# LayerNorms 2 and 3 with statistics from transposed token blocks, and two sets of first weights split at an earlier place in the program

## The chip, the cores and the metric

The kernel runs on one core of a Trainium2 chip. The metric is the time of one execution on the device in microseconds (us). Before the change the median of three runs is 2775.86 us (2774.26 to 2776.49).

## The reference, cut to what matters

One encoder layer is applied to two groups of 512 tokens (prompt and sample) with shared weights, model width 1024, all in fp32:

```
x = LN1(alpha*x + 0.5*SwiGLU_1(x))
h = x @ W_in                                  # columns for MLA, RWKV-7 and gates
A = MLA(h) @ P_mla ;  B = RWKV7_bidir(h) @ P_rwkv
x = LN2(alpha*x + (sig(g_A)*A + sig(g_B)*B) @ W_o)
x = LN3(alpha*x + CrossAttn(x, LN(mem)))
x = LN4(alpha*x + 0.5*SwiGLU_2(x))

def _layernorm(x, g, b):
    mu = mean(x, -1); var = mean((x - mu)**2, -1)
    return (x - mu) * rsqrt(var + 1e-5) * g + b
```

A LayerNorm needs the mean and variance of each token over its 1024 features.

## The kernel before, in words

**Layout.** Activations lie transposed: features on the 128 partitions, 512 tokens along a row. A group's activation is eight rows (`KT` = 8) of 128 x 512. Each fp32 operand of a product is split into a high part, rounded to fp32r by ScalarE (a CAST, line 246), and a low part, the difference, made by VectorE or GpSimd (line 247, which the profile shows as L180 where VectorE is called through the wrapper `Held`). A product is three matmuls of 128x128 by 128x512 (`Bank.prod`, matmuls at L216): high x high, high x low, low x high. Results collect in eight PSUM banks, four with tag `a`, two with `b`, two with `c`. Tile names in the profile: `xh`, `xl` are the parts of normalized rows, `wraw` a raw weight slot, `whl` its two parts, `wt` a sum of weight blocks, `ps` a bank, `cc` the constants with the identity.

**Weights.** The projections and everything up to the cross-attention output read their weights from a `Stream`. `Stream.fetch` takes a raw buffer (pool `w`: 2 buffers) and a split buffer (`whl`, pool `w`: 3 buffers, one more in another pool), issues a load of 512 KB on SP's queue (L142) and the two split instructions. `next_slot` calls `fetch` when a slot is asked for and none is ready. The feed-forward's weights come from `FfnWeights`, a generator with the same buffers; `next()` keeps up to `AHEAD` = 3 tiles of lead, and `ahead(n)` runs the generator n steps before they are asked for (loads at L459). The first feed-forward uses it while the input is loaded.

**Order.** The program is written as one list of instructions. A planner lays down each engine's order before the run: it keeps a model of time, and of the instructions whose inputs and buffers the model has ready it takes the one that stands first in the program. So a later line can run ahead of an earlier one, and each engine then works through its own list in that order. `order(...)` adds an edge by hand; `k.after`, set by `BlockNorm.stats(..., True)`, puts all later VectorE instructions behind the end of that statistic.

**The stages around the change, in order of time.**

1. *First feed-forward* (`ffn`). Its last loop, `down_step` over `DOWN`, makes seven block products a step by Strassen's scheme. The last step (`final`) takes its products in the order 1 2 6 5 3 7 4; `ahead(i)` is called before the i-th.
2. *LayerNorm 1* is a `BlockNorm`. `add(half)` handles four rows: for each of four token blocks, four transposes of 128 x 128 on TensorE into one bank (L221), then one `bn_stats` on VectorE over the bank. `stats` joins the halves (`bn_aggr`), makes the reciprocal root by three Newton steps of small VectorE instructions (`rstd_of`), and `spread` brings scale and shift back to the transposed layout by eight transposes. `applying` then does, for each row: multiply and add on VectorE, gain and bias on ScalarE (L359), high part on ScalarE, low part on GpSimd.
3. *Projections.* `compressed(2, ..., decay)` takes three weight slots and runs them abreast: for each row of a group the nine matmuls of the three slots, first group 0, then group 1. At its end ScalarE copies the banks (L1002).
4. Recurrence, attention and their outputs.
5. *LayerNorm 2* over `mix_row`, and *LayerNorm 3* over `out_rows`. Both are `RowNorm`: after each row ScalarE squares it (L375), VectorE adds the square to one sum (`ln_s`), and GpSimd (group 0, L378) or VectorE (group 1) adds the row to another. `stats` reduces the two sums over the partitions by eight fp32 matmuls with a column of 1/1024 (`k.mean`; the profile has sixteen records a group).
6. Cross attention: `both(attend(1), out_rows(0))` interleaves group 1's attention with group 0's output rows; `out_rows(1)` follows, then the rows of LayerNorm 3.
7. *Second feed-forward*: the same `ffn` with `last=True`. It asks for its first four weight slots by `fw.next()`, and runs them abreast over group 0's rows of LayerNorm 3, then over group 1's.

Of the kernel before, what the change touches and what calls it, by code (L numbers as in the profile page):

```python
# [11 lines left out]
F32 = mybir.dt.float32  # L12
F32R = mybir.dt.float32r
I32 = mybir.dt.int32
AF = mybir.ActivationFunctionType
ALU = mybir.AluOpType
# [4 lines left out]
P = 128  # L21
# [342 lines left out]
            yield  # L364


class RowNorm(Norm):


    def add(self, n):  # L370
        nc, y = self.k.nc, self.y(n)
        if n == 0:
            self.s1, self.s2 = self.tile("ln_s1", 2), self.tile("ln_s2", 2)
        sq = self.tile("sq", 4) if n else self.s2
        nc.scalar.activation(out=sq, in_=y, func=AF.Square)  # L375
        if n:
            eng = nc.gpsimd if self.tags[0] == "c" else nc.vector
            eng.tensor_tensor(out=self.s1, in0=self.s1 if n > 1 else self.y(0), in1=y, op=ALU.add)  # L378
            nc.vector.tensor_tensor(out=self.s2, in0=self.s2, in1=sq, op=ALU.add)

    def stats(self):
        k, nc, sb = self.k, self.k.nc, self.sb
        st = Bank(k, self.tags[0])
        for o, t in enumerate((self.s1, self.s2)):
            for b in range(4):
                st.mm(st.t[:, 4 * o + b : 4 * o + b + 1], t[:, b * P : b * P + P], k.mean)
        m = sb.tile([P, 3, 4], F32, name="ln_m", tag="ln_m", bufs=2)
        mean, var, sq = m[:, 0], m[:, 1], m[:, 2]
        nc.vector.tensor_copy(m[:, 0:2], st.t[:, 0:8].rearrange("p (a b) -> p a b", b=4))
        nc.vector.scalar_tensor_tensor(out=sq, in0=mean, scalar=-1.0, in1=mean, op0=ALU.mult, op1=ALU.mult)  # L390
        nc.vector.scalar_tensor_tensor(out=var, in0=sq, scalar=LN_EPS / ALPHA**2, in1=var, op0=ALU.add, op1=ALU.add)
        Norm.spread([self], mean, var)


class BlockNorm(Norm):


# [129 lines left out]
            ra, rb = nxt  # L527


def ffn(k, fw, x32, std, rows_of, op_tile, posts, sums, d_h, d_s, norm_of, applied, last=False):  # L530

# [50 lines left out]
    def down_step(n, u2, u4):  # L584
        m, p0, p1_ = DOWN[n]

        def ahead(i):

            if i == 2 and m == 3:
                while due:  # L590
                    due.pop(0)()
            if i == 2:
                for p in range(p1_, max([p1_, *(b for _, _, b in DOWN[n + 1 : n + 2])])):
                    fetch(p)

        ps, done = {}, set()
        y = {(r, c): x32[:, rows_of[r], 2 * m + c] for r in range(2) for c in range(2)}

        def add(out, name, u):
            nc.vector.scalar_tensor_tensor(out=out, in0=ps[name].t, scalar=SC, in1=u, op0=ALU.mult, op1=ALU.add)  # L600

        final = n == len(DOWN) - 1

        def more(r, c, u):

            eng = nc.vector if final else nc.gpsimd
            eng.tensor_tensor(out=y[r, c], in0=y[r, c], in1=u, op=ALU.add)  # L607

        def to_y(r, c, name, u):
            add(y[r, c], name, y[r, c])  # L610
            if not final:
                more(r, c, u)

        def summed(i, x):

            x.add(m // 2)
            if m == 3 and not last:
                if i == 1:  # L620
                    going.append(applied(rows_of[0], norms[0]))
                    for _ in range(3):
                        next(going[0])
                BlockNorm.stats([x], True)
            elif m == 3 and i == 1:
                BlockNorm.stats(norms, True)

        todo = [
            ("p1", "1", lambda: nc.scalar.activation(out=u2, in_=ps["1"].t, func=AF.Identity, scale=SC)),
            ("c11", ("2", "p1"), lambda: to_y(0, 0, "2", u2)),  # L630
            ("u2", ("6", "c11"), lambda: add(u2, "6", u2)),
            ("u4", ("5", "u2"), lambda: add(u4, "5", u2)),
            ("u3", ("7", "u4"), lambda: add(u2, "7", u2)),
            ("c22", ("7", "u4"), lambda: to_y(1, 1, "7", u4)),
            ("c12", ("3", "u4"), lambda: to_y(0, 1, "3", u4)),
            ("c21", ("4", "u3"), lambda: to_y(1, 0, "4", u2)),
        ]
        if final:
            for name, (r, c, of, u) in {"d11": (0, 0, "p1", u2), "d12": (0, 1, "u4", u4), "d22": (1, 1, "u4", u4),
                                        "d21": (1, 0, "u3", u2)}.items():  # L640
                todo.insert(0, (name, (of,), lambda r=r, c=c, u=u: more(r, c, u)))
            todo = [(a, (*b, "d" + a[1:]) if a[0] == "c" else b, f) for a, b, f in todo]
        if p1_ == NP and m == 3:
            for r, x in enumerate(norms):
                todo.append((f"n{r}", (f"c{r + 1}1", f"c{r + 1}2"), lambda r=r, x=x: summed(r, x)))
        elif p1_ == NP and m == 1:
            due.extend(lambda r=r, x=x: summed(r, x) for r, x in enumerate(norms))
        strassen(k, fw, turn_of(n), ps, done, todo, p1_ - p0,
                 lambda o, i: tuple(slot(OPS.index(o), (p0 + i) % 4)[:, j] for j in range(2)), ahead)


    with posts() as sb:
# [13 lines left out]
        for g in range(G):  # L666
            xp = [std[g].pair(i) for i in range(KT)]
            banks = [Bank(k, "a") for _ in range(4)]
            ws = [[(o[0][:, i * P : i * P + P], o[1][:, i * P : i * P + P]) for i in range(KT)] for o in w]
            if last:  # L670
                abreast(banks, ws, xp)
            for j in range(2):
                pg, pu = banks[2 * j : 2 * j + 2]
                if not last:
                    for b, o in zip((pg, pu), ws[2 * j : 2 * j + 2]):
                        b.prod(b.t, list(zip(o, xp)))
                s = sb.tile([P, 2, T], F32, name="s", tag="s", bufs=2)[:, 0]
                nc.scalar.activation(out=s, in_=pg.t, func=AF.Silu)
                nc.vector.tensor_tensor(out=s, in0=s, in1=pu.t, op=ALU.mult)
                to_h(s, d_s[j][g], sb)  # L680
# [122 lines left out]
def kernel(  # L803
# [55 lines left out]
    nc.vector.memset(k.ones, 1.0)  # L859
    k.half = cp.tile([P, 1], F32, name="half")  # L860
    nc.vector.memset(k.half, 0.5)
    k.mean = cp.tile([P, 1], F32, name="mean")
    nc.vector.memset(k.mean, 1.0 / D)
    vc = cp.tile([P, NVEC], F32, name="vc")
    nc.sync.dma_start(out=vc, in_=vec)

# [31 lines left out]
    with ExitStack() as f1:  # L898
# [35 lines left out]

        places = {n: (xpools[0], "x", 4) for n in ("A11", "A12")}
        places.update({n: (xpools[1], "x", 4) for n in ("A22", "S4")}, **{n: (xo, "xo", 6) for n in ("S1", "S2", "S3")})
        ffn(k, fw, x32, xs, (0, 1), op_tiles(places), lambda: pool("post1"), sums1, d_h, d_s, norm1, applied1)

    def gate_out(n, g, h, t):
        nc.scalar.activation(out=t, in_=h, func=AF.Tanh, scale=0.5, bias=hbg[:, n : n + 1])  # L940
# [364 lines left out]
    y32 = keep.tile([P, G, KT, T], F32, name="x32")  # L1305
    x32 = [y32[:, g] for g in range(G)]

    def norms_of(i):
        return [RowNorm(k, sb, lambda n, g=g: x32[g][:, n], f"ln{i}_g", f"ln{i}_b", "cb"[g] * 2) for g in range(G)]

    for q in range(4):
        for g in range(G):
            nc.sync.dma_start(out=x32[g][:, 2 * q : 2 * q + 2], in_=d_x1[g][:, 2 * q : 2 * q + 2])
    wb_pool = cross.enter_context(pool("wb", "right"))
    st.use((wp, 3, 2), (wb_pool, 2, 0), (wp, 3, 2), (wb_pool, 2, 0), (wp, 3, 2))

    def sum_row(norm, g, n, b, f):
        y = x32[g][:, n]
        nc.vector.scalar_tensor_tensor(out=y, in0=b.t, scalar=f, in1=y, op0=ALU.mult, op1=ALU.add)
        norm.add(n)  # L1320

    norms = norms_of(2)
    w = []

    def mix_row(g, n):
# [4 lines left out]
    for n0 in (0, 4):  # L1330
        w += [st.blocks(KT) for _ in range(4)]
        for g in range(G):
            for n in range(n0, n0 + 4):
                mix_row(g, n)
            if (n0, g) == (4, 0):
                norms[0].stats()
    x2 = [None, None]
    for g in range(G):
        if g:
            norms[g].stats()  # L1340
        x2[g] = (acts if g else others)(KT, "x")
        norms[g].apply(x2[g])

# [79 lines left out]
    kvs[1] = memory_of(1)  # L1423
    xo[1] = acts(4, "co")
    w = [st.blocks(4) for _ in range(KT)]
    norms = norms_of(3)
    both(attend(1), out_rows(0))
    norms[0].stats()
    for _ in out_rows(1):
        pass  # L1430
    x3 = [None, None]
    for g in range(G):
        if g:
            norms[g].stats()
        x3[g] = acts(KT, "x")
        norms[g].apply(x3[g])


    cross.close()
    ow, of = ctx.enter_context(pool("ow", "right")), ctx.enter_context(pool("of"))  # L1440
    fw = FfnWeights(k, wf2, [(wp, 3)] * 3 + [(ow, 1)], [(wp, 2)] * 2 + [(ow, 1)], ow)
    ln = []

    def sums2():
# [8 lines left out]

    places = {n: (mixed, "xs", 8) for n in ("A11", "A12", "A22", "S4")}
    places.update({n: (keep, "xs", 4) for n in ("S1", "S2")}, S3=(of, "xo", 2))
    ffn(k, fw, y32, x3, (1, 0), op_tiles(places), lambda: pool("post2"), sums2, d_h, d_s, norm4, applied4, True)


def softmax(k, sb, s, scale):
# [544 lines left out]
```

## Time and profile before

| what | value |
|---|---|
| median of three runs | 2775.86 us |
| the profiled execution, its time | 2775.84 us |
| its span, first to last instruction | 2774.1 us |
| mean granted TensorE clock | 0.963 |
| TensorE busy | 2605.6 us, 94% |
| VectorE busy | 2123.8 us, 77% |
| ScalarE busy | 1095.9 us, 40% |
| GpSimd busy | 699.1 us, 25% |

The profiled execution agrees with the median to 0.02 us, and its span is 1.7 us shorter than its time. In the rows below, a timeline row gives the start in us from the span's start, the duration, the engine (PE = TensorE, DVE = VectorE, ACT = ScalarE, POOL = GpSimd, SPq = SP's queue), the line, the operation, output and inputs, shapes, and the count of merged instructions; brackets give how long the engine stood before it and what ended that. A group row gives busy us and the mean ns of one, then idle time before it. A matmul's duration includes its way through the array: in a dense stream the next one starts before it ends, so costs on TensorE are read from starts.

### The profile page before, as it was taken

Reading aid. Unit: us, or ns where it says so; the run is one execution under the profiler, and the core shown is the slowest. Engines: PE = TensorE matmul, PEld = TensorE weight load, DVE = VectorE, ACT = ScalarE, POOL = GpSimd, SP = SyncE. Lnnn points to the kernel's source line nnn. Section 1 sums busy time; section 2 is a strip of 40 time slices with the busy share of each in tenths; the row PEclk is TensorE's granted clock in tenths of the full one; section 3 lists DMA queues with packets and bytes.
Section 4 is the critical chain, followed back from the end, with each engine's and each line's share of the span. In section 5 each row is a group of like instructions: output and inputs, shape, how many; then the busy total and the mean of one; then the engine's idle time right before and its main releaser. Section 6 shows DMA issues by size and latency. Waiting matters only on the chain.

```text
span 2774.1 us, 41500 instructions
## 1 busy us (share of the span) xinstructions
PE 2605.6 (94%) x15600; PEld 2079.9 (75%) x15600; DVE 2123.8 (77%) x3749; ACT 1095.9 (40%) x2008; POOL 699.1 (25%) x479
## 2 busy tenths in 40 slices
PE   8999999997899999997989888899999999999996
PEld 7888887785767777776777676677777888887784
DVE  7888887999366777758475768656798888887987
ACT  5334342223353555444443432224554343342222
POOL 0323332443100001133133321103032332332443
PEclk9999999999989999998899898999999999999998
DMA  4344437661244333343434354441101433447751
GB/s 171 130 150 160 152 145 296 235 235 57 95 165 150 112 106 111 111 143 129 131 109 131 119 178 126 161 174 42 54 31 67 161 144 138 152 162 267 273 202 68
DMA packets 164776, 398.18 MB, mean 144 GB/s; under 512 B 41120, under 2 KB 47520, under 8 KB 164576
## 3 DMA queue, kind: packets, MB, share of 16 engines
q1 hardware_dynamic: 164576, 395.53, 40.8%
q8 instruction: 124, 2.03, 0.3%
q14 instruction: 76, 0.62, 0.1%
HBM read 261.50 MB, written 133.96 MB: 143 GB/s over the span
## 4 chain that ended last, share of the span: by engine, by line
PE 76%; DVE 15%; ACT 3%; issue 2%; DMA 2%; POOL 1%; SPq 0%; POOLq 0%; ACTq 0%; DVEq 0%
PE ps L216 73%; PE ps L221 3%; DVE whl L180 2%; DVE dw L180 2%; DVE z L180 1%; DVE x L180 1%; DVE tm L180 1%; DVE rs L180 1%; DVE wt L180 1%; DVE s L180 1%; DVE ln_s L180 1%; DVE phi L180 1%; ACT whl L246 0%; DMA ld<-d_rw 0%; DVE up L180 0%
## 5 line engine op out<-in xcount | busy, mean ns | idle before, releaser
L216 PE MATMUL ps<-xh,whl 128*128 128x512 f32 x2688 | 890.2, 402 | 26.7 <-DVE whl L180 16.8
L216 PE MATMUL ps<-xo,whl 128*128 128x512 f32 x3792 | 899.7, 396 | 14.2 <-DVE z L180 8.5
L216 PEld LDWEIGHTS ps<-xo,whl 128*128 128x128 f32 x3792 | 713.0, 189 | 185.6 <-DVE z L180 6.7
L216 PEld LDWEIGHTS ps<-xh,whl 128*128 128x128 f32 x2688 | 507.8, 190 | 144.2 <-DVE whl L180 20.4
L216 PE MATMUL ps<-xl,whl 128*128 128x512 f32 x1344 | 535.1, 399 | 1.5 <-POOL xl L247 1.5
L180 DVE TENSOR_TENSOR whl<-wraw,whl 128x512 fp32r<-128x512 f32 (+4 forms) x273 | 282.5, 1045 | 63.6 <-ACT whl L246 62.9
L246 ACT CAST whl<-wraw 128x512 fp32r<-128x512 f32 (+4 forms) x318 | 223.9, 715 | 250.1 <-PE ps L216 210.8
L216 PEld LDWEIGHTS ps<-xl,whl 128*128 128x128 f32 x1344 | 255.8, 190 | 55.8 <-POOL xl L247 2.3
L709 POOL TENSOR_TENSOR s<-s,up 128x512 f32<-128x512 f32 x80 | 115.9, 1449 | 626.6 <-DVE up L180 391.1
L246 ACT CAST whl<-wt 128x512 fp32r<-128x512 f32 (+3 forms) x280 | 148.5, 555 | 276.0 <-PE ps L216 164.1
L180 DVE TENSOR_TENSOR whl<-wt,whl 128x512 fp32r<-128x512 f32 (+3 forms) x280 | 216.7, 795 | 10.8 <-ACT whl L246 10.3
L247 POOL TENSOR_TENSOR whl<-wraw,whl 128x1024 fp32r<-128x1024 f32 x45 | 109.1, 2426 | 385.5 <-ACT whl L246 355.4
L246 ACT CAST hop<-s 128x512 fp32r<-128x512 f32 x128 | 79.5, 621 | 238.2 <-POOL s L709 178.0
L180 DVE TENSOR_TENSOR hop<-s,hop 128x512 fp32r<-128x512 f32 x128 | 121.4, 949 | 55.4 <-ACT hop L246 48.0
L180 DVE SCALAR_TENSOR_TENSOR x<-ps,x 128x512 f32<-128x512 f32 x184 | 124.5, 683 | 50.6 <-PE ps L216 50.2
L180 DVE TENSOR_TENSOR wt<-wraw 128x512 f32<-128x512 f32 (+3 forms) x140 | 110.6, 791 | 1.0
L180 DVE TENSOR_TENSOR wt<-wraw,wt 128x512 f32<-128x512 f32 (+3 forms) x140 | 103.1, 737 | 4.2 <-DMA wraw<-in_wf_dram 2.1
L607 POOL TENSOR_TENSOR x<-x,s 128x512 f32<-128x512 f32 x48 | 70.7, 1478 | 129.4 <-DVE x L180 129.4
L247 POOL TENSOR_TENSOR xl<-x,xh 128x512 fp32r<-128x512 f32 x48 | 68.6, 1453 | 91.8 <-ACT xh L246 91.5
L180 DVE TENSOR_TENSOR p<-ps,p 128x512 f32<-128x512 f32 x120 | 82.2, 685 | 7.8 <-PE ps L216 4.8
L607 POOL TENSOR_TENSOR x<-x,z 128x512 f32<-128x512 f32 x48 | 71.3, 1486 | 52.8 <-DVE x L180 49.2
L216 PE MATMUL ps<-mh,whl 128*128 128x512 f32 x256 | 82.2, 401 | 0.0
(328 smaller groups left out, 3728.2 us busy)
## 6 DMA issues: line engine op xcount, KB each, us to landing
d_h<-hop SPq DMA_DIRECT2D x140, 512.0 KB, 2.6
xo<-d_h SPq DMA_DIRECT2D x140, 512.0 KB, 7.2
wraw<-in_wf_dram SPq DMA_DIRECT2D x95, 512.0 KB, 3.4
wraw<-in_wa_dram SPq DMA_DIRECT2D x57, 512.0 KB, 3.5
wraw<-in_wb_dram SPq DMA_DIRECT2D x36, 512.0 KB, 3.4
wraw<-in_wf_dram SPq DMA_DIRECT2D x36, 384.0 KB, 3.9
ld<-d_rw SPq DMA_DIRECT2D x24, 512.0 KB, 4.7
d_gate<-t SPq DMA_DIRECT2D x32, 256.0 KB, 2.4
```

Source lines behind the costliest of these rows:

```text
L180: inst = f(*args, **kw)
L216: self.last = order(k.tc, k.nc.tensor.matmul(out, a, b, start=start, stop=stop), self.last)
L221: self.last = order(self.k.tc, self.k.nc.tensor.transpose(out, a, ident), self.last)
L246: nc.scalar.copy(hi, src)
L247: (low or nc.vector).tensor_tensor(out=lo, in0=src, in1=hi.bitcast(F32), op=ALU.subtract)
L607: eng.tensor_tensor(out=y[r, c], in0=y[r, c], in1=u, op=ALU.add)
L709: nc.gpsimd.tensor_tensor(out=s[:, i], in0=s[:, i], in1=up[:, i], op=ALU.mult)
```

## The change

`RowNorm` is removed, and `norms_of` makes `BlockNorm`s with bank tags for transposes and spreading. The rows call `add` once for each four rows. In the first feed-forward's last step, before its fifth product, `early` fetches the first three slots of the projections' stream. The second feed-forward's `FfnWeights` and the pool `ow` are made before `out_rows(1)`, and three of its four first slots are generated after the fourth, sixth and eighth row of group 1. `ffn`'s flag `last` becomes `early`, with the opposite sense.

```diff
-class RowNorm(Norm):
-    def add(self, n):
...
-    def stats(self):
...
-def ffn(k, fw, x32, std, rows_of, op_tile, posts, sums, d_h, d_s, norm_of, applied, last=False):
+def ffn(k, fw, x32, std, rows_of, op_tile, posts, sums, d_h, d_s, norm_of, applied, early=None):
...
+        final = n == len(DOWN) - 1
+
         def ahead(i):
 
             if i == 2 and m == 3:
                 while due:
                     due.pop(0)()
+            if i == 4 and final and early:
+                early()
...
-            if m == 3 and not last:
+            if m == 3 and early:
...
-            if last:
+            if not early:
                 abreast(banks, ws, xp)
...
-    k.mean = cp.tile([P, 1], F32, name="mean")
-    nc.vector.memset(k.mean, 1.0 / D)
...
-        ffn(k, fw, x32, xs, (0, 1), op_tiles(places), lambda: pool("post1"), sums1, d_h, d_s, norm1, applied1)
+        ffn(k, fw, x32, xs, (0, 1), op_tiles(places), lambda: pool("post1"), sums1, d_h, d_s, norm1, applied1,
+            lambda: [st.fetch() for _ in range(3)])
...
-    def norms_of(i):
-        return [RowNorm(k, sb, lambda n, g=g: x32[g][:, n], f"ln{i}_g", f"ln{i}_b", "cb"[g] * 2) for g in range(G)]
+    def norms_of(i, *tags):
+        return [BlockNorm(k, sb, lambda n, g=g: x32[g][:, n], f"ln{i}_g", f"ln{i}_b", tags[g]) for g in range(G)]
...
+    ow = ctx.enter_context(pool("ow", "right"))
...
-        norm.add(n)
-
-    norms = norms_of(2)
+        if n % 4 == 3:
+            norm.add(n // 4)
+
+    norms = norms_of(2, ("c", "b"), ("c", "c"))
...
-                norms[0].stats()
+                BlockNorm.stats(norms[:1], False)
...
-            norms[g].stats()
+            BlockNorm.stats(norms[1:], False)
...
-    norms = norms_of(3)
+    norms = norms_of(3, ("a", "b"), ("c", "c"))
     both(attend(1), out_rows(0))
-    norms[0].stats()
-    for _ in out_rows(1):
-        pass
+    BlockNorm.stats(norms[:1], False)
+    fw = FfnWeights(k, wf2, [(wp, 3)] * 3 + [(ow, 1)], [(wp, 2)] * 2 + [(ow, 1)], ow)
+    for i, _ in enumerate(out_rows(1)):
+        if i % 4 == 3 and i > 4:
+            fw.ahead(1)
...
     cross.close()
-    ow, of = ctx.enter_context(pool("ow", "right")), ctx.enter_context(pool("of"))
-    fw = FfnWeights(k, wf2, [(wp, 3)] * 3 + [(ow, 1)], [(wp, 2)] * 2 + [(ow, 1)], ow)
+    of = ctx.enter_context(pool("of"))
```

More of the change, by code (lines that the diff above doesn't have):

```diff
@@ L364, in applying @@
             yield
-class RowNorm(Norm):
-    def add(self, n):
[L371 to L379, printed above, removed]
-    def stats(self):
[L382 to L392, printed above, removed]
 class BlockNorm(Norm):
@@ L600, in add @@
             nc.vector.scalar_tensor_tensor(out=out, in0=ps[name].t, scalar=SC, in1=u, op0=ALU.mult, op1=ALU.add)
-        final = n == len(DOWN) - 1
         def more(r, c, u):
@@ L673, in ffn @@
                 pg, pu = banks[2 * j : 2 * j + 2]
-                if not last:
+                if early:
                     for b, o in zip((pg, pu), ws[2 * j : 2 * j + 2]):
@@ L1433 @@
         if g:
-            norms[g].stats()
+            BlockNorm.stats(norms[1:], False)
         x3[g] = acts(KT, "x")
@@ L1455 @@
     places.update({n: (keep, "xs", 4) for n in ("S1", "S2")}, S3=(of, "xo", 2))
-    ffn(k, fw, y32, x3, (1, 0), op_tiles(places), lambda: pool("post2"), sums2, d_h, d_s, norm4, applied4, True)
+    ffn(k, fw, y32, x3, (1, 0), op_tiles(places), lambda: pool("post2"), sums2, d_h, d_s, norm4, applied4)
 def softmax(k, sb, s, scale):
```

## The prediction

> **What bounds the kernel now.** I read the page first (busy times, chain), then the waits of TensorE, then the timelines of each engine at the four places that the diff touches, then windows for the granted clock.
>
> ```profile
> span 2774.1 us, 41500 instructions
> PE 2605.6 (94%) x15600; PEld 2079.9 (75%) x15600; DVE 2123.8 (77%) x3749; ACT 1095.9 (40%) x2008; POOL 699.1 (25%) x479
> ...
> PE 76%; DVE 15%; ACT 3%; issue 2%; DMA 2%; POOL 1%; SPq 0%; POOLq 0%; ACTq 0%; DVEq 0%
> ...
> PE ps L216 <- DVE whl L180: 18.9, 5, 14.3
> ```
>
> TensorE is busy 94% of the span and makes 76% of the chain that ended last. So time is won only where TensorE stands, and each instruction put on TensorE in a dense stretch costs its full spacing. The last row is of the waits: five waits of matmuls for a weight split on VectorE are 18.9 us, and one of them is 14.3 us. It lies at the start of the projections:
>
> ```profile
> 678.35 0.40 PE L216 MATMUL ps<-xl,whl 128*128 128x512 f32 x1
> 684.45 1.09 PE L221 MATMUL ps<-cc,ln_v 128*128 128x128 f32 x4 [5.70 <-DVE ln_v L180]
> ...
> 700.71 1.22 PE L216 MATMUL ps<-xh,whl 128*128 128x512 f32 x2 [14.32 <-DVE whl L180]
> ...
> 638.07 14.53 SPq L142 DMA_DIRECT2D wraw<-in_wa_dram  x2
> 700.68 0.33 SPq L142 DMA_DIRECT2D wraw<-in_wa_dram  x1
> ...
> 661.82 1.05 ACT L246 CAST whl<-wraw 128x1024 fp32r<-128x1024 f32 x1 [7.96 <-PE ps L216]
> ...
> 699.37 1.29 DVE L180 TENSOR_TENSOR whl<-wraw,whl 128x1024 fp32r<-128x1024 f32 x1
> ...
> 701.18 1.70 DVE L180 TENSOR_TENSOR whl<-wraw,whl 128x1024 fp32r<-128x1024 f32 x1
> ...
> 688.43 18.08 POOL L247 TENSOR_TENSOR xl<-x,xh 128x512 fp32r<-128x512 f32 x13 [5.72 <-ACT xh L246]
> ...
> 734.52 0.59 ACT L1002 COPY c<-ps 128x512 f32<-128x512 f32 x1 [10.59 <-PE ps L216]
> ```
>
> Two of the first three weight slots were loaded from 638, and the second was cast by 662.9. Yet their low halves are made on VectorE only at 699.37 and 701.18, among the last rows of LayerNorm 1, and the third slot is loaded only then, since it reuses the raw buffer of the first. The normalized rows are there much earlier: GpSimd makes the low halves of the last thirteen rows from 688.43 on, 1.39 us each (18.08/13). Row 3 of the first token group is complete at 689.8, and the last row of the second at 706.5. The copy at 734.52 tells when the first three projections (3 slots x 16 rows x 3 = 144 matmuls) ended, at 734.4.
>
> ```profile
> 640.00:678.00 38.00, 31.22 (x167) 24.61 (x166) 35.38 (x65) 6.93 (x10) 9.76 (x6) 1.00 0.07 24
> 680.43:704.33 23.90, 5.41 (x15) 3.90 (x16) 22.07 (x40) 17.16 (x28) 18.10 (x14) 0.50 0.47 184
> 707.00:740.00 33.00, 32.52 (x142) 26.49 (x142) 8.76 (x12) 10.53 (x17) 0.21 (x2) 1.00 0.20 65
> 1895.58:1898.99 3.41, 3.41 (x10) 2.63 (x9) 2.11 (x13) 0.00 (x0) 0.00 (x0) 0.50 0.00 0
> 2062.83:2076.49 13.66, 10.99 (x34) 8.10 (x34) 13.23 (x27) 4.05 (x7) 5.66 (x3) 0.50 0.43 136
> ```
>
> In these windows the columns are TensorE, weight loads, VectorE, ScalarE, GpSimd, then granted clock. Where TensorE stood, the clock fell to 0.50 and stayed there for some us after work came back. In the dense window 142 matmuls take 33 us, 0.233 us each.
>
> The second place is the start of the second feed-forward:
>
> ```profile
> 2059.15 0.39 PE L216 MATMUL ps<-xh,whl 128*128 128x512 f32 x1
> ...
> 2062.12 2.96 PE L216 MATMUL ps<-mean,ln_s 128*128 128x1 f32 x16 [0.35 <-DVE ln_s L180]
> 2066.47 2.00 PE L216 MATMUL ps<-xh,whl 128*128 128x512 f32 x3 [1.39 <-DVE whl L180]
> ...
> 2096.20 0.50 PE L216 MATMUL ps<-xh,whl 128*128 128x512 f32 x1 [0.28 <-DVE s L180]
> ...
> 2048.10 1.05 ACT L246 CAST whl<-wraw 128x1024 fp32r<-128x1024 f32 x1 [0.92 <-PE ps L216]
> ...
> 2064.39 0.68 DVE L180 TENSOR_TENSOR s<-s,ps 128x512 f32<-128x512 f32 x1
> ...
> 2065.20 1.22 DVE L180 TENSOR_TENSOR whl<-wraw,whl 128x1024 fp32r<-128x1024 f32 x1
> ...
> 2073.16 1.23 DVE L180 TENSOR_TENSOR whl<-wraw,whl 128x1024 fp32r<-128x1024 f32 x1
> ...
> 2116.23 0.69 DVE L180 TENSOR_TENSOR s<-s,ps 128x512 f32<-128x512 f32 x1 [9.83 <-PE ps L216]
> ```
>
> The same picture, smaller. The first group's 4 x 24 = 96 matmuls need 22.4 us, but run from 2059.15 to 2096.20, 37 us. The second slot's cast was done at 2049.2; the four low halves came on VectorE from 2065.20 to 2074.4, behind the rows of group 0 (until 2065.1) and between the links of group 1's statistics.
>
> **The change, part by part.**
>
> *Transposed blocks (LayerNorms 2 and 3).* The trace has their price at LayerNorm 1, which does just this:
>
> ```profile
> L221 PE MATMUL ps<-cc,x 128*128 128x128 f32 x64 | 9.7, 277 | 2.8 <-DVE ln_b L180 2.1 <-DVE x L180 0.7
> L180 DVE BATCH_NORM_STATS2 ln_b<-ps 128x6 f32<-128x512 f32 x16 | 10.6, 689 | 0.7 <-PE ps L221 0.6
> ...
> 657.14 0.60 PE L221 MATMUL ps<-cc,x 128*128 128x128 f32 x4
> 657.50 0.95 PE L216 MATMUL ps<-xo,whl 128*128 128x512 f32 x3
> 658.29 0.38 PE L221 MATMUL ps<-cc,x 128*128 128x128 f32 x2
> ...
> 1892.48 1.05 PE L216 MATMUL ps<-mean,ln_s 128*128 128x1 f32 x8 [0.57 <-POOL ln_s L378]
> 1893.39 0.47 PE L216 MATMUL ps<-ml,whl 128*128 128x512 f32 x1
> ...
> 1894.17 0.95 PE L216 MATMUL ps<-mean,ln_s 128*128 128x1 f32 x8
> 1894.98 0.47 PE L216 MATMUL ps<-ml,whl 128*128 128x512 f32 x1
> ...
> L180 DVE TENSOR_TENSOR ln_s<-ln_s,sq 128x512 f32<-128x512 f32 x28 | 28.0, 1001 | 5.8 <-ACT sq L375 5.5
> ```
>
> Four transposes of one bank hold TensorE from 657.14 to 657.50, 0.36 us; the three matmuls behind them take 0.79 instead of 0.70. So a bank costs 0.45 us. A LayerNorm of two groups fills 16 banks: 7.2 us, or 14.4 for both. What goes is the sums by matmul: 0.91 + 0.81 us of stream, two restarts of 0.09 and the wait of 0.57, so 2.5 us for this group. I take the same for group 1: 4.9 for LayerNorm 2. Its net is +2.3. In LayerNorm 3, group 0 pays 3.6 and saves 1.9, group 1's first half pays 1.8, and the second half lies in the stall counted below. Together +5.8, say **+6**, on the dense path. Bounds: +1 (the 1.7 us of the half-clock window that follows those sums at 1895.58 goes too, and waits with them) to +11 (also the idle 2.8/16 us a bank, and no saving in LayerNorm 3).
>
> VectorE loses 28 additions of 1.0 us and the twelve of group 1's first sum, and gets 32 statistics of 0.69 us (22 us) and 16 small ones. ScalarE loses 32 squares, GpSimd its sums. None of these bounds the dense stretch, so nothing there, covered by TensorE. The memset of `k.mean` at the start goes: nothing, beside the first loads.
>
> The trace calls a transpose 277 ns long, three times its spacing. The Trainium skill, page "TensorE: Matmul & The Clock Gate", section "Part 4: PE-mode transpose", gives about 275 ns in a kernel's context, which agrees as a duration. Were it occupancy, 128 of them would cost 35 us instead of 14.4 and the whole sum would be +3 us, 2778; the starts at 657.14 and 657.50 decide against it.
>
> *Projections' weights.* `early` issues three loads and six split halves at the fifth of the last step's seven products, so ahead of LayerNorm 1 in program order. Nothing is added; each is moved past the last sums, both statistics, sixteen rows and, on SP, the eight stores of d_x1. VectorE is busy 35.38 of 38 us in 640:678, so the low halves cost there: two of 1.2 us fit partly in its 2.6 idle us; the third needs a buffer that the last products hold, comes near 674 and delays the rows by 1.2. I take 1.7 us of delay for the rows (bounds 0 and 3.7, three whole splits). The three casts find ScalarE busy 6.93 of those 38 us. On SP the loads pass stores that are read back only in the recurrence's filling work: nothing, even if the third load's wait for a raw buffer holds them. The VectorE time freed at 699.37 to 702.9 goes to the last rows.
>
> What is late next: the rows. The three slots run abreast, nine matmuls a row, 2.1 us, slower than rows arrive (1.39). The 27 matmuls of rows 0 to 2 run before 689; the other 117 start when row 3 is there, 689.8 + 1.7 = 691.5, and need 27.3 us, 718.8. One clock window at half (1.7) and one bank turnover (0.6) make 721. Against 734.4 that is **-13**. Bounds: -16 (no delay, full clock) and -7 (3.7 us delay and two more half-clock windows).
>
> *Second feed-forward's weights.* Three of the four slots are split in program order within group 1's output rows. The first two follow their casts, the third still waits for the last row's matmul to free its buffer. VectorE between 2041 and 2060 drops fourteen additions of 0.6 us spacing, gains four statistics and two splits of 1.2: about 4 us less, so group 0's rows end near 2061 instead of 2065.1. Then TensorE has 48 matmuls (11 us) for two slots at 2059.15 and the rest as they come: 2059.15 + 22.4 + 1.8 (four banks) + 0.8 (eight spreads) = 2084.2; with 1 us of waits 2085.2 against 2096.2, **-11**. Bounds: -12 and -5 (VectorE stays behind, clock stays at half). Is it given back by the operand sums on VectorE? It idles 9.83 us before 2116.23, so 11 us less on TensorE and about 5 us less on its own side still fit. The `ow` pool opened earlier is space, no time.
>
> *Sum.* +6 - 13 - 11 = -18 us. The profiled execution took 2775.84, as the median 2775.86: **2757.8**. 0.2%, 5.6 us, is about what a measurement of this kernel tells from no change.
>
> **Rivals.**
> 1. *Only one of the two starts is won.* For: each engine's order is laid down before the run, and splits already sit far behind their casts (661.82 to 701.18). Against: both now stand ahead of the norms in the program. -13 + 6 gives 2769, -11 + 6 gives 2771.
> 2. *Slower: the banks stall TensorE.* Most norms rotate two banks, each freed by a 0.69 us statistic. If TensorE stood 0.9 us for each of the 28 banks in dense stretches: +25, 2783. It decides from (18 + 5.6)/28 = 0.84 us a bank; against it, 2.8 us of idle stood before 16 banks in LayerNorm 1, 0.18 each.
> 3. *Clock.* A burst of small instructions drops the clock: the half-speed window at 1895.58 comes right after sixteen of them. One window costs 1.7 us; seven dense half-norms, 12 us: 2770. Against: 64 transposes in 640:678 at clock 1.00. The same section of that page says that transposes do not count as busy for the clock; the 640:678 window does not bear it out.
> 4. *The splits stay where they were* (the change does not do what it says): +6, 2782.
> 5. *More*: both starts and the norms at their good bounds, -16 - 12 + 1 = -27, 2749; half of it 2752.
>
> **How the numbers follow.** Forecast 0.62 (own range 2753 to 2766), rival 1 0.14, rival 2 0.05, rival 3 0.05, rival 4 0.04, rival 5 0.10. Faster by over 0.2% (below 2770.3): the forecast, rival 5, half of rivals 1 and 3, 0.81. Slower (above 2781.4): rivals 2 and 4, less 0.01, 0.08. Same 0.11. The range 2750 to 2771 leaves out rivals 2 and 4, parts of 1 and 3 and the end of 5.
>
> **What would show it.** Right: no wait near 14 us before the first projections, their 144 matmuls ending 13 us sooner after the last product; low halves on VectorE before LayerNorm 1's rows; group 0 of the second feed-forward in about 26 us instead of 37, at clock 1.0; 128 more transposes, dense stretches of LayerNorms 2 and 3 about 6 us longer. Wrong: splits still among the rows; gaps of 0.8 us before transposes; half-clock windows inside LayerNorm 2; a new wait for operand sums after the feed-forward's first blocks.

## The result, and the profile after

| | median, us | runs, us | ratio to the kernel before |
|---|---|---|---|
| before | 2776.18 | 2774.26 to 2776.51 | |
| after | 2747.59 | 2745.05 to 2753.66 | 0.9902 [0.9884, 0.9919] |

The change wins 28.6 us where 18 were forecast; the median lies 2.4 us below the range. The profiled execution is the slowest of its four, 2753.66 us (22.2 us won), so stages are compared below over several kernels' traces, too.

The page of the changed kernel, its span, busy times and the shares of the chain that ended last:

```profile
span 2751.4 us, 41550 instructions
...
PE 2601.3 (95%) x15664; PEld 2085.6 (76%) x15664; DVE 2113.7 (77%) x3746; ACT 1075.5 (39%) x1976; POOL 677.1 (25%) x465
...
PE 54%; DVE 11%; issue 3%; ACT 3%; DMA 2%; POOL 1%; SPq 1%; POOLq 0%; ACTq 0%; DVEq 0%
```

TensorE is busy for about as many us as before. The start of the projections, in the timeline, its waits and a window (columns as in the prediction):

```profile
661.75 1.21 DVE L180 TENSOR_TENSOR whl<-wraw,whl 128x1024 fp32r<-128x1024 f32 x1
666.04 1.23 DVE L180 TENSOR_TENSOR whl<-wraw,whl 128x1024 fp32r<-128x1024 f32 x1
676.47 1.21 DVE L180 TENSOR_TENSOR whl<-wraw,whl 128x1024 fp32r<-128x1024 f32 x1
...
690.08 0.62 PE L221 MATMUL ps<-cc,ln_v 128*128 128x128 f32 x4 [0.92 <-DVE ln_v L180]
694.03 0.97 PE L216 MATMUL ps<-xh,whl 128*128 128x512 f32 x3 [1.04 <-ACT xh L246]
712.48 0.98 PE L216 MATMUL ps<-xh,whl 128*128 128x512 f32 x2 [2.48 <-ACT xh L246]
...
724.84 0.59 ACT L977 COPY c<-ps 128x512 f32<-128x512 f32 x1 [4.53 <-PE ps L216]
...
PE ps L216 <- DVE whl L180: 3.3, 2, 2.8
...
690.00:718.00 28.00, 24.01 (x98) 18.68 (x99) 22.31 (x31) 18.96 (x31) 17.05 (x15) 0.94 0.44 162
```

The low halves stand ahead of LayerNorm 1's rows, the wait of 14.3 us is gone, and the copy that stood at 734.52 stands at 724.84. (The 2.8 us left in that list of waits lie elsewhere.) The start of the second feed-forward:

```profile
2030.66 1.23 DVE L180 TENSOR_TENSOR whl<-wraw,whl 128x1024 fp32r<-128x1024 f32 x1
2037.60 1.21 DVE L180 TENSOR_TENSOR whl<-wraw,whl 128x1024 fp32r<-128x1024 f32 x1
2047.34 2.27 DVE L180 TENSOR_TENSOR whl<-wraw,whl 128x1024 fp32r<-128x1024 f32 x1
2050.13 1.95 DVE L180 TENSOR_TENSOR whl<-wraw,whl 128x1024 fp32r<-128x1024 f32 x1
...
2048.44 0.48 PE L216 MATMUL ps<-xh,whl 128*128 128x512 f32 x1
2052.13 0.97 PE L216 MATMUL ps<-xh,whl 128*128 128x512 f32 x3 [0.50 <-DVE whl L180]
2074.90 0.50 PE L216 MATMUL ps<-xh,whl 128*128 128x512 f32 x1 [0.71 <-ACT s L654]
2077.36 0.50 PE L216 MATMUL ps<-xh,whl 128*128 128x512 f32 x1 [0.80 <-DVE s L180]
...
2048.00:2075.00 27.00, 25.61 (x122) 20.15 (x120) 26.13 (x51) 14.70 (x22) 11.36 (x9) 1.00 0.12 39
```

The row that stood at 2096.20 before (a wait for `s`) is the one at 2077.36. From the first product it comes 28.9 us later (2077.36 - 2048.44) instead of 37.1 (2096.20 - 2059.15), and the clock stays at 1.00. In both traces 102 products lie in that stretch, group 0's 96 and six of group 1. The 96 alone took 35.2 us before (the 97th starts at 2094.35) and 25.6 now (they end at 2074.0; the 97th is the one at 2074.90).

The next table shows how far each trace is ahead of the kernel before, in us. It compares the starts of the same instructions of VectorE, ScalarE, GpSimd and of the DMA issues, before minus now, as the median over those that started in the 20 us from the time named (in the time of the kernel before). In column 2020, where ScalarE's rows changed their order, the value is VectorE's. The runs e0 to e14 are described below.

| from | 640 (last step of FFN 1) | 740 (projections) | 1440 | 1820 (recurrence over) | 1920 (LN 2 over) | 2020 (attention over) | 2100 (FFN 2 under way) | 2760 (end) |
|---|---|---|---|---|---|---|---|---|
| after | -2.2 | 9.7 | 13.4 | 9.9 | 10.3 | 12.5 | 18.6 | 22.6 |
| e0, the same kernel | -1.1 | 13.4 | 15.4 | 11.5 | 12.6 | 14.9 | 21.0 | 24.9 |
| e5, without the splits ahead | -1.0 | 15.5 | 19.3 | 18.5 | 19.9 | 22.2 | 28.1 | 30.7 |
| e6, after with the old places | -0.5 | 16.1 | 16.0 | 18.9 | 18.7 | 20.6 | 26.5 | 26.3 |
| e10, norms alone, old places | -2.7 | -2.7 | -1.7 | -6.4 | -6.3 | -4.3 | 1.2 | 0.8 |
| e2, early projections alone | -0.7 | 15.4 | 16.9 | 10.7 | 11.1 | 12.7 | 11.3 | 11.1 |

Read across, the same steps recur: 12 to 17 us at the projections' start where `early` is in; 5.5 to 6.1 us between 2020 and 2100 wherever the norms are in; about 2 us in the attention, but 1.6 in e2 as well, which has the old norms; and 2.6 to 4 us within the second feed-forward in after, e0 and e5, but not in e6 and e10. Between 1440 and 1820 the traces move by -6.2 to +2.9 in no order that follows the change: the same program moved by -3.5 (after) and -3.9 (e0). The cause of that scatter stays open.

### The profile page after: what moved, and what is told of

Read it like the earlier page. It is cut to its first block, busy times and chain, and to the rows that moved or that the text cites. A ratio compares the mean times of both kernels' runs of the same rounds, so it can differ in the third digit from the quotient of the medians.

```text
span 2751.4 us, 41550 instructions
## 1 busy us (share of the span) xinstructions
PE 2601.3 (95%) x15664; PEld 2085.6 (76%) x15664; DVE 2113.7 (77%) x3746; ACT 1075.5 (39%) x1976; POOL 677.1 (25%) x465
## 4 chain that ended last, share of the span: by engine, by line
PE 54%; DVE 11%; issue 3%; ACT 3%; DMA 2%; POOL 1%; SPq 1%; POOLq 0%; ACTq 0%; DVEq 0%
PE ps L216 51%; PE ps L221 3%; DVE whl L180 1%; DVE z L180 1%; DVE dw L180 1%; DVE x L180 1%; DVE tm L180 1%; DMA ld<-d_rw 1%; DVE rs L180 1%; DVE phi L180 1%; DVE gm L180 1%; DVE wt L180 0%; ACT whl L246 0%; DVE s L180 0%; POOL ln_z L358 0%
## 5 line engine op out<-in xcount | busy, mean ns | idle before, releaser
L216 PEld LDWEIGHTS ps<-xh,whl 128*128 128x128 f32 x2688 | 509.7, 191 | 131.0 <-ACT xh L246 13.8
```

The source lines that it names most:

```text
L216: self.last = order(k.tc, k.nc.tensor.matmul(out, a, b, start=start, stop=stop), self.last)
```

## The experiments

First theory (A): the mechanism is as forecast, and single terms are mis-sized, above all the +6 of the transposes. Rivals: the +6 holds and the starts won more (B); it is a matter of how single executions run (L).

**e0**, the changed kernel again, no edit.

> The changed kernel once more, unchanged, for its size beside -18. Theory A (the change's terms were mis-sized, above all the +6 of the transposes): -28 us again, within 2, and the profiled execution no slower than the others. Rival L (the extra 10 us are a matter of how single executions run: first loads, clock, spacing of the matmuls): the median comes back to -18 to -23.

Measured 2747.16 us, 0.9892 [0.9879, 0.9906]: 29.5 us less than the kernel before on that chip. L falls. That its profiled execution would be no slower than the others did not come true: it was the slowest again, 2751.34.

**e1**, norms only:

```diff
-            lambda: [st.fetch() for _ in range(3)])
+            lambda: None)
...
-    for i, _ in enumerate(out_rows(1)):
-        if i % 4 == 3 and i > 4:
-            fw.ahead(1)
+    for _ in out_rows(1):
+        pass
```

with `ow` and `FfnWeights` made where the kernel before made them.

> Only LayerNorms 2 and 3 from transposed blocks; both weight starts as before. Theory A (transposes cost less than the waits and the half-clock window that go with the old sums): -1 to -5 us against the kernel before, and no half-clock window within LayerNorm 2. Rival B (the +6 holds and the two starts won more than 13 and 11): +4 to +8. The prediction's own step: +6.

2764.24 us, 0.9949 [0.9936, 0.9961], -12.4 us: more than any theory allowed. The part that was to cost 6 us won about as much as either start was to (13 and 11).

**e2**, the kernel before with `early` alone:

```diff
+            if i == 4 and n == len(DOWN) - 1 and early:
+                early()
...
+            early=lambda: [st.fetch() for _ in range(3)])
```

> The kernel before with the projections' three first slots fetched in the last feed-forward step and nothing else. The prediction's step: -13 (bounds -16 to -7). Theory A, from the two traces: -14 to -16, with no 14 us wait and the copy of the first products near 724. Rival B: -18 or more.

2764.77 us, 0.9953 [0.9941, 0.9966], -11.9 us: within the prediction's bounds, short of theory A's -14 to -16. Its trace gains 16.1 us between 640 and 740, but loses 6.2 us again between 1440 and 1820.

**e4**, norms and splits ahead, without `early` (the first two lines of e1's edit).

> The changed kernel without the early fetch for the projections, so norms and second feed-forward's splits. The prediction's steps: +6 - 11 = -5. Theory A: -10 to -14, of which the splits ahead of time make 8 to 11 beside the norms alone, and the 14.3 us wait for a weight split at the projections is there again. Rival B: +6 - 13, so -7 or less.

2763.67 us, 0.9953 [0.9940, 0.9967], -13.0 us. The total fits theory A, its parts do not: over e1 the splits ahead add 0.6 us, within the measurement, not 8 to 11.

Two new theories then. **V**: the second feed-forward's start was held by VectorE's queue and by the statistics' links, not by the place of the splits. **P**: part of the gain is where tiles lie in SBUF. Below is a dense stretch of each feed-forward, one without any wait (first window in the first feed-forward, second in the second; TensorE alone, and the clock after it):

```profile
100.00:400.00 300.00, 300.00 (x1305) 1.00 0.40 149
2130.00:2430.00 300.00, 300.00 (x1282) 1.00 0.39 144
```

That is the kernel before; the changed one:

```profile
100.00:400.00 300.00, 300.00 (x1308) 1.00 0.41 151
2130.00:2430.00 300.00, 300.00 (x1293) 1.00 0.41 152
```

In 300 us of unbroken matmuls at clock 1.00 TensorE issues 1282 before (234.0 ns each) and 1293 after (232.0). Nothing of the change reaches into that loop. But `k.mean`, which the change drops, is a constant in front of all tiles of SBUF's left side, and constants take places of 32 bytes: all left tiles lie 32 bytes lower. Laying the compiled programs' addresses beside the traces, matmul for matmul, the mean spacing before another 512-column matmul is 234.2 ns where the moving operand lies 1664 bytes past a multiple of 2048 (left side, before), 232.6 at 1632 (left side, after), and about 228 at 2016 (right side, both). The weights lie at 2016 plus multiples of 512 in both.

**e5**, the changed kernel without the splits ahead (e1's edit, its last part).

> The changed kernel without the splits ahead of the second feed-forward: norms and early projections' weights only. The prediction's steps: the whole change gives this plus -11, so about 11 us slower than the changed kernel. Theory V (that stall was VectorE's queue and the statistics' chain, which the norms alone cure; the placing of the splits is worth nothing): within 1.5 us of the changed kernel, -27 to -29 us against the kernel before, and group 0 of the second feed-forward dense without the splits ahead.

2747.45 us, 0.9889 [0.9873, 0.9904], the same as the whole change (2747.16 and 2747.59), and 30.3 below the kernel before on that chip, a little more than V's 27 to 29. Its timeline at the second feed-forward's start:

```profile
2034.56 1.22 DVE L180 TENSOR_TENSOR whl<-wraw,whl 128x1024 fp32r<-128x1024 f32 x1
2036.29 2.27 DVE L180 TENSOR_TENSOR whl<-wraw,whl 128x1024 fp32r<-128x1024 f32 x1
2041.33 1.21 DVE L180 TENSOR_TENSOR whl<-wraw,whl 128x1024 fp32r<-128x1024 f32 x1
2043.77 1.17 DVE L180 TENSOR_TENSOR whl<-wraw,whl 128x1024 fp32r<-128x1024 f32 x1
...
2038.64 0.48 PE L216 MATMUL ps<-xh,whl 128*128 128x512 f32 x1
2041.46 0.44 PE L221 MATMUL ps<-cc,x 128*128 128x128 f32 x2 [1.19 <-DVE x L180]
2067.84 0.50 PE L216 MATMUL ps<-xh,whl 128*128 128x512 f32 x1 [0.80 <-DVE s L180]
```

With the old place in the program the splits still begin 4.1 us ahead of the first product (2034.56 against 2038.64; in the kernel before 6.1 behind it). The wait for `s` comes 29.2 us after that product, with the splits ahead 28.9. The norms alone cure this start: group 0's 96 products take 25.9 us.

**e6**, the changed kernel with the old places: 32 unused bytes, as the mean's place was.

```diff
+    k.pad = cp.tile([P, 8], F32, name="pad")
+    nc.vector.memset(k.pad, 0.0)
```

> The changed kernel with one unused 32-byte constant put back where the mean's was, so that all tiles of the left side of SBUF lie again at multiples of 64 bytes instead of 32 above them. Theory P (the place of the moving operand in SBUF sets the spacing of dense matmuls: in the two first traces 234.2 ns at a multiple of 64 bytes, 232.6 ns at 32 above it, for 5264 matmuls of 512 columns): +8 us against the changed kernel, -20 against the kernel before, and the second feed-forward's dense stretch back at 234.3 ns. Rival S (the faster spacing comes from what the norms do, the other engines' traffic among it): no change, -28.

2754.68 us, 0.9910 [0.9896, 0.9923], 7 us above the changed kernel (P expected 8), and the dense stretch is back at 1283 matmuls:

```profile
2130.00:2430.00 300.00, 300.00 (x1283) 1.00 0.41 150
```

**e7**, the kernel before with the same two lines.

> The kernel before with one more unused 32-byte constant and nothing else: its left tiles then lie 32 bytes above a multiple of 64. Theory P: -8 us, second feed-forward's dense stretch at 232 to 233 ns instead of 234.3. Rival S: 0 us.

2771.86 us, 0.9978 [0.9969, 0.9987], -5.9 us from an unused constant. P holds, with 5.9 us for its 8, and S falls. At 1696 bytes past a multiple of 2048 the spacing is 233.3 ns, not the 232.6 of 1632, though both are 32 past a multiple of 64: the place within 64 bytes isn't the rule.

**e8**, the changed kernel with `[P, 96]` for the pad (384 bytes).

> The changed kernel with an unused constant of 384 bytes, so that 8736 of the 9344 matmuls of 512 columns read their moving operand from 2016 bytes past a multiple of 2048, as the right side's do already (228.0 ns there in the first traces; left side 232.6 at 1632 past it). Theory P with the place within 2048 bytes as the cause: 4656 matmuls x 4.6 ns = -21 us against the changed kernel, near 2726 us. If only the place within 64 bytes counts (theory P64): no change, 2747. If the side or pool counts and not the place: no change either.

2732.09 us, 0.9828 [0.9815, 0.9842]: 15 us less than the changed kernel where 21 were expected; why not all of it came is open. Both feed-forwards run at 226 ns (300/1325):

```profile
100.00:400.00 300.00, 300.00 (x1325) 1.00 0.42 151
2130.00:2430.00 300.00, 300.00 (x1325) 1.00 0.42 151
```

**e10**, norms only at the old places (e1 with e6's two lines).

> Norms only (LayerNorms 2 and 3 from transposed blocks), with one unused 32-byte constant in the place of the mean's, so that the tiles lie where they lay before. The prediction's step: +6 against the kernel before. Theory V (no price is left: the links that go give back more than the transposes take, 6 us of it at the second feed-forward's start): -4 to -8. Norms alone without that constant were -12.4.

2770.39 us, 0.9975 [0.9966, 0.9985], -5.9 us (-9.4 to -4.2 by the interval). This is the price of the norms alone.

**e3b**, the kernel before with the splits ahead alone:

```diff
-        sq = self.tile("sq", 4) if n else self.s2
+        sq = self.tile("sq", 1) if n else self.s2
...
+    ow = ctx.enter_context(pool("ow", "right"))
...
-    for _ in out_rows(1):
-        pass
+    fw = FfnWeights(k, wf2, [(wp, 3)] * 3 + [(ow, 1)], [(wp, 2)] * 2 + [(ow, 1)], ow)
+    for i, _ in enumerate(out_rows(1)):
+        if i % 4 == 3 and i > 4:
+            fw.ahead(1)
...
```

> The kernel before with the second feed-forward's weights split within group 1's output rows, and nothing else of the change; for the space, the squares of the old LayerNorms share one buffer instead of four. The prediction's step: -11. Theory V (VectorE's queue of additions and the statistics' links hold that start, not the place of the splits): -2 to +2, and the second feed-forward's first group still waits within its products.

2778.16 us, 1.0004 [0.9993, 1.0015]: nothing won. One buffer of squares costs some 2.7 us in LayerNorm 2 by its trace, so the splits alone are worth about 1 us by the medians and under 5 by the interval; what the one buffer costs in LayerNorm 3 was not separated. Its timeline:

```profile
2054.76 1.72 DVE L180 TENSOR_TENSOR whl<-wraw,whl 128x1024 fp32r<-128x1024 f32 x1
2059.31 1.21 DVE L180 TENSOR_TENSOR whl<-wraw,whl 128x1024 fp32r<-128x1024 f32 x1
2070.52 1.21 DVE L180 TENSOR_TENSOR whl<-wraw,whl 128x1024 fp32r<-128x1024 f32 x1
2077.72 1.60 DVE L180 TENSOR_TENSOR whl<-wraw,whl 128x1024 fp32r<-128x1024 f32 x1
...
2067.91 0.39 PE L216 MATMUL ps<-xh,whl 128*128 128x512 f32 x1
2071.79 0.73 PE L216 MATMUL ps<-xh,whl 128*128 128x512 f32 x2 [0.28 <-DVE whl L180]
2086.55 0.65 PE L221 MATMUL ps<-cc,ln_m 128*128 128x128 f32 x4 [0.87 <-DVE ln_m L180]
2101.09 0.79 PE L216 MATMUL ps<-xh,whl 128*128 128x512 f32 x1 [5.73 <-ACT s L678]
```

The first two splits now stand 13 and 9 us ahead of the first product and the wait for weights shrinks to 0.28. Group 0's 96 products take 27.3 us, 35.2 in the kernel before, so V's expectation that this group would still wait within its products hardly came true. But group 1's scale (`ln_m`) reaches TensorE 18.6 us after the first product (2086.55 - 2067.91; 14.0 in the kernel before), and a new wait of 5.73 us stands at the end of group 0, for a bank that ScalarE has yet to empty (`s`): ScalarE is at group 1's late rows until 2099.1. With the old statistics the earlier splits hand the wait on.

**e11**, the transposes of LayerNorms 2 and 3 done twice:

```diff
-            for i in range(4):
+            for i in list(range(4)) * (2 if self.g[:3] in ("ln2", "ln3") else 1):
```

> The changed kernel with every transpose of LayerNorms 2 and 3 done twice into the same place: 128 transposes more, nothing else. The prediction's price of 0.45 us a bank of four, or 0.36 without the restart of the stream: +10 to +14 us against the changed kernel. If a transpose's 277 ns were occupancy: +35. If the transposes lie in time in which TensorE would wait anyway: +0 to +5.

2761.01 us, 0.9943 [0.9929, 0.9957], 13.8 above e0: 128 transposes at 0.108 us, 0.43 a bank. Sixteen of them in the timeline, and the matmul behind them:

```profile
1884.96 1.91 PE L221 MATMUL ps<-cc,x 128*128 128x128 f32 x16
1886.62 0.48 PE L216 MATMUL ps<-mh,whl 128*128 128x512 f32 x1
```

1.66 us for sixteen, 104 ns each. The price of 0.45 us a bank was right; 277 ns of occupancy, which would have been 35 us, is excluded.

**e12**, the changed kernel with 352 bytes of pad on the left and a first tile of 32 bytes in a pool of its own on the right.

> The changed kernel with 352 bytes of unused constant on the left side of SBUF and 32 on the right, so that 8736 matmuls read their moving operand from 1984 bytes past a multiple of 2048, and the weights lie 32 bytes lower as well. Theory P-absolute (the distance of the moving operand from a multiple of 2048 sets the spacing): spacings between those at 2016 (226.7 ns) and 1664 (234.3), so 2735 to 2770. Theory P-relative (moving operand and weights must lie alike): 226.7 ns and about 2732 again. Theory P64 (a multiple of 64 bytes is bad): 234 ns everywhere, also in the first feed-forward's first products, 2790 or more.

2733.89 us, 0.9838 [0.9821, 0.9854], with 1326 and 1325 matmuls in the two windows: P-relative.

**e13**, as e12 with 32 bytes on the left and 352 on the right, so that operands and weights lie where the left operands of the kernel before lay.

> The changed kernel with 32 bytes of unused constant on the left side of SBUF and 352 on the right: moving operands of 8736 matmuls and the weights all lie 1664 bytes past a multiple of 2048, where the left side's operands of the kernel before lay. Theory P-relative (the spacing is short where moving operand and weights lie alike): 226.7 ns in both feed-forwards, 2732 to 2734 us. Theory P-absolute (1664 past is a bad place by itself): 234.3 ns in both, with the first feed-forward's first products too: about 2790.

2731.48 us, 0.9835 [0.9821, 0.9848]:

```profile
span 2728.3 us, 41553 instructions
...
100.00:400.00 300.00, 300.00 (x1325) 1.00 0.41 152
2130.00:2430.00 300.00, 300.00 (x1325) 1.00 0.41 151
```

The place that gave 234 ns with weights at 2016 gives 226 with weights at 1664. P-absolute, which said 2790, falls: what counts is how the moving operand lies against the weights. e13 and e8 beat both kernels of the change.

**e14**, the kernel before with 352 bytes of pad on the left, nothing else.

> The kernel before with 352 bytes of unused constant on the left, so that its operands lie as its weights do (2016 past a multiple of 2048), and nothing else. Theory P-relative and P-absolute both: 4656 matmuls x (234.2 - 227.4 ns) = -32 us at the most, -20 to -26 by what the changed kernel gained beyond its own place (2747 to 2732, and 7 before that): 2750 to 2756. If the gain needs the changed norms: 2776.

2753.40 us, 0.9911 [0.9896, 0.9926], -24.0 us. With aligned operands the change is then worth 21 to 22 us (from e14's 2753.4 to e8's 2732.1 or e13's 2731.5), with the old places 21.5 to 23 (from 2776.2 or, on e6's chip, 2777.8 to e6's 2754.7).

## Why the prediction was right and wrong

**The step that failed is the one costed in half a sentence:** "The memset of `k.mean` at the start goes: nothing, beside the first loads." The instruction is indeed nothing. The 32 bytes under it are 7 us (e6), without which the change ends at 2754.68 us, inside the range. No row quoted in the prediction shows it. The trace of the kernel before had a sign: at clock 1.00, 300 us hold 1305 matmuls in the first feed-forward and 1282 in the second, where the prediction read 0.233 us as one price for all.

**+6 for the transposes.** The gross price held: 0.43 us a bank measured, 0.45 forecast. The net did not: -5.9 (e10). So against 13.8 us of transposes about 20 us came back, where the prediction counted 8 to 9. "None of these bounds the dense stretch, so nothing there" failed, on what leaves VectorE, 28 additions of 1.0 us among it: matmuls waited behind that work. In the attention eight matmul waits for `sm_p`, in the list of waits of the kernel before (and of e2, with the old norms), become two:

```profile
PE ps L221 <- DVE sm_p L180: 2.4, 8, 0.6
```

The same row of e10:

```profile
PE ps L221 <- DVE sm_p L180: 1.0, 2, 0.6
```

The traces with the new norms win about 2 us in the attention. Most of it is a half-clock window of the profiled kernel before, which e2, with the old norms, does not have there either:

```profile
1957.02:1960.43 3.41, 3.41 (x12) 0.50 0.07 26
```

So these waits are worth under 1 us, and the 5.5 to 6.1 us come at the second feed-forward's start. LayerNorm 2 came out between 0.2 us lost and 1.4 won, where a loss of 2.3 was forecast: the bound of +1 named the half-clock window at 1895.58, and this went as the bound said (clock 1.00 over LayerNorm 2 in the changed kernel, below).

```profile
1820.00:1930.00 110.00, 109.25 (x509) 88.10 (x508) 58.50 (x108) 29.26 (x41) 19.06 (x14) 1.00 0.25 90
```

**-11 for the second feed-forward's start.** The net of the stage was near, 6 us against the forecast 7.5 (11 less 3.5 of LayerNorm 3), but it does not come from the splits that were moved. Late splits did hold group 0 as the prediction read, and its 96 products came down from 35.2 us to 25.6, as the forecast 26 said. (The 37 us of the prediction include six products of group 1.) By estimate from the windows of the kernel before, some 4 us of the loss was idle time (37.05 - 32.96 from 2059.15 to 2096.20) and 5.5 us half clock (half of the 10.99 busy us in 2062.83:2076.49). But the norms alone give the same: 25.9 us in e5 and 26.0 in e10, with the splits at their old place in the program. The splits alone give 27.3 us in e3b, and there the time is lost again at group 0's end. The likely reason is that the planner takes what is ready first in program order, and with the old sums gone VectorE reaches the splits in time wherever they stand. What share of the cure belongs to the 28 additions and what to the shorter statistics was not tested. Two waits that the forecast did not have follow group 0 (0.71 and 0.80 us, for ScalarE and VectorE to empty the banks).

**-13 for the projections' start.** Mechanism and place right, size near the good bound: 16.5 us in e5's trace (-1.0 to 15.5), 16.5 between the medians of e4 and e0. Its rows:

```profile
691.85 0.96 PE L216 MATMUL ps<-xh,whl 128*128 128x512 f32 x3 [1.07 <-ACT xh L246]
693.21 0.50 PE L216 MATMUL ps<-xl,whl 128*128 128x512 f32 x1 [0.40 <-POOL xl L247]
...
691.88 17.33 POOL L247 TENSOR_TENSOR xl<-x,xh 128x512 fp32r<-128x512 f32 x13 [5.72 <-ACT xh L246]
...
702.80 1.51 DVE L180 TENSOR_TENSOR whl<-wraw,whl 128x1024 fp32r<-128x1024 f32 x1
...
719.00 0.59 ACT L977 COPY c<-ps 128x512 f32<-128x512 f32 x1 [4.87 <-PE ps L216]
...
690.00:718.00 28.00, 26.13 (x112) 20.39 (x111) 18.21 (x29) 20.47 (x34) 17.97 (x15) 1.00 0.44 169
```

From 691.85 to the copy are 27.2 us, the forecast's 27.3 for 117 matmuls; the half-clock window (1.7) and the bank turnover (0.6) that it added did not come. The rows' low parts were later than the forecast 1.7 us: they begin at 691.88 instead of 688.43, 2.4 us late beyond the 1.0 that this trace was behind. But the first products of a row read its high part, so TensorE started only 1.0 us later than row 3 was complete before (691.85 against 689.8, less that 1.0). The profiled execution after lost some of this again in the wait of 2.48 us at 712.48. The split of a low half ahead of the last row, 1.51 us at 702.80 in e5, is much longer there:

```profile
704.99 5.28 DVE L180 TENSOR_TENSOR whl<-wraw,whl 128x1024 fp32r<-128x1024 f32 x1
```

It takes 5.28 us in e0 as well and 5.26 in e12, but 1.50 to 1.53 in e2, e5, e6, e8, e11 and e13. What lengthens it is open.

**The rivals.** In LayerNorms 2 and 3 of the changed kernel no stall on banks and no half-clock window was seen; matmuls stand between the transposes there, so this tells nothing of transposes alone. A half-clock window is left ahead of the projections (680.04:686.87, clock 0.50), after TensorE had stood idle for 2.80 us. Rival 5, more, was the nearest in size, not in cause. Rival 4 was half true in a way not thought of: the second splits might as well have stayed in their old place.

Terms, forecast and measured: norms +6 and -5.9 (e10); projections -13 and -16.5; second splits -11 and 0; places 0 and -7. They sum to -18 and -29.4. The measured ones come from runs with different other parts, so that the sum agrees with 28.6 only roughly. Two errors of 11 to 12 us cancelled between norms and splits, which was luck. By itself `early` gave 11.9 us (e2), 4.6 less than on top of the norms; whether that is the scatter of the recurrence or a real dependence is not settled.

## What to carry to other kernels

Work that leaves an engine which bounds nothing is not free of effect: look at which waits end on that engine before costing its removal at zero, and undo each part alone, since a right sum can hide two wrong causes. Before a gain is put down to a change, compare at equal addresses: a dropped 4-byte constant was worth 7 us here, and padding until operands and weights lay alike as much as 24 (352 bytes in e14).

## What was not expected of the hardware

In unbroken streams of fp32r matmuls (128x128 by 128x512) at granted clock 1.00 the spacing depends on how the moving operand's address stands to the weights'. It is 226.7 ns in the second feed-forward's dense stretch where the two are a multiple of 512 bytes apart (three placements: 1664, 1984 and 2016 past a multiple of 2048). Modulo 2048 the weights of that stretch lie 0, 512, 1024 and 1536 bytes from the operand in about equal numbers, and in e8, e12 and e13 each of the four distances gives 226.7 ns. The spacing is 232.5, 234.3 and 233.3 ns where the operand lies 384, 352 and 320 bytes below such a place. Distances between were not tried in a dense stretch; the profile shows no wait for it, only the count of matmuls in a window. The Trainium skill, page "TensorE: Matmul & The Clock Gate", section "Wait — 56ns, not 53.3ns?", gives 215.7 ns from start to start for matmuls of 512 columns once the clock is up. None of the dense stretches compared here reaches it; the best is 11 ns above.
